# Input stage of a two-layer decoder trunk: the first pair of k-tiles in single pieces, the gain vectors on the other queue, the bias row later, the keys' scales first

## The chip, the cores and the metric

The kernel runs on one core of a Trainium2 chip. The metric is the device time of one execution in microseconds (us). Of the kernel before there are three timed runs and one profiled execution; all times below come from these.

## The reference, cut to what matters

The program is a decoder trunk on one sequence of 256 tokens with 1024 features: a DSA layer (an indexer scores the keys, the best 64 are kept, attention runs over a shared latent), an MLP, an NSA layer and a second MLP. Only its first lines bear on the change:

```
h = rmsnorm(x, g_attn[0])                 # x: 256 tokens x 1024 features
proj = h @ w_in                           # 1024 x 456
c_q, c_kv, k_idx, w_idx = split(proj, [256, 384, 448])
c_q, c_kv, k_idx = rmsnorm of each, with its own gain
rel   = relu(q_idx . k_idx)               # 8 indexer heads, queries x keys
score = sum over heads of w_idx * rel     # causal; the top 64 keys are kept
logits = q_abs . c_kv + rel_bias[bucket(distance)]   # attention, softmax
```

The norm's factor per token is applied after the product, so the kernel multiplies the raw x (times the gain of each feature) with `w_in` and scales the result later.

## The kernel before, in words

All tensors lie in SBUF in tiles of 128 partitions. The stream is held transposed (`xT`: 128 features of a k-tile on the partitions, 8 k-tiles, 256 tokens), so `w_in` is used in 8 k-tiles of 128 x 456, which arrive in four pairs (`win_raw`, 456 KB a pair; `xT`, 256 KB a pair). The result stands in two PSUM banks, `proj[0]` and `proj[1]`, one for each half of the tokens.

The first pair (j = 0) is multiplied in plain fp32: ScalarE (ACT) makes `xg` = `xT` times the gain, and TensorE (PE) runs four matmuls of 128 x 456, each of which it carries out in two passes. The pairs 1 to 3 are multiplied in split form: ACT rounds `xT` to `xgh` and `w_in` times the gain to the high half of `win`, VectorE (DVE) forms the remainders `xgl` and the low half of `win`, and PE runs three passes of 128 x 456 for each of four combinations, 12 a pair, 36 in all. The gains and some other columns lie in `vec` (26 KB).

Beside this, ACT squares `xT` into `sqs`, DVE adds the four squares, GpSimd (POOL) the last two halves (`Sx`): these are the sums for the norm of x. Behind the adds DVE copies `proj`'s first columns to `zc`, PE transposes them (`tz`), and the indexer's queries follow (`qi`). From sums of squares of `proj` (`ss`) POOL raises all scales to the power -1/2 (`scs`: column 0 for the query latent, 1 for the key latent, 2 for the indexer's keys, 3 for the norm of x). The scaled keys (`kd`, DVE) are transposed by PE (`tk`) and copied with their gain (`kiT`, DVE); PE forms the indexer's scores (`ix`), ACT cuts them at zero (`rel`), and DVE adds them up with the weights `widx` (`score`) and finds the top 64 in a long chain of MAX and MATCH_REPLACE.

The bias row is a side branch: `relb` (32 x 8) and a one-hot table `oneh` (32 x 256) are loaded on ACT's DMA queue, PE multiplies them (`ups`), DVE copies the result to `usb`, ACT's queue writes it to DRAM (`udr`), and SyncE's queue (SP) reads it back in 1 KB rows as `biasT` (1 MB), which the attention needs much later. Ahead of all products PE runs ten matmuls on a tile of ones (`warm_ps`).

The order of instructions on each engine is set by a scheduler that works on estimated times; `pin` keeps an instruction in program order among the pinned ones of its engine, `behind(a, b)` places a after b. DMA is issued by two queues, SP's and ACT's, and an issue may have to wait for a buffer: `raw` tiles come from a pool of five.

Of the kernel before, what the change touches and what calls it, by code (L numbers as in the profile page):

```python
# [22 lines left out]
F32 = mybir.dt.float32  # L23
F32R = mybir.dt.float32r
AF = mybir.ActivationFunctionType
OP = mybir.AluOpType
# [4 lines left out]
P, T, D, KT = 128, 256, 1024, 8  # L31
H, G, R, HD = 8, 2, 4, 128
# [4 lines left out]
NEG = -1e30  # L37
# [5 lines left out]
V_GA, V_GM, V_GKV, V_GF, V_GQ, V_GKVL, V_GKI = 0, 16, 32, 40, 48, 50, 51  # L43
# [7 lines left out]
def trunk(ctx: ExitStack, tc: tile.TileContext, I, out):  # L51
    nc = tc.nc
    const = ctx.enter_context(tc.tile_pool(name="const", bufs=1))
    big = ctx.enter_context(tc.tile_pool(name="big", bufs=10))
    rawp = ctx.enter_context(tc.tile_pool(name="raw", bufs=5))
# [12 lines left out]
    dram = ctx.enter_context(tc.tile_pool(name="dr", bufs=1, space=DRAM))  # L68

    def bank(name, acc=False):  # L70
        if acc:
            return psA.tile([P, 512], F32, tag="acc", name=name)
        return psB.tile([P, 512], F32, tag="ps", name=name)

    def bigt(shape, dt, name):
        return big.tile(shape, dt, tag="big", name=name)

    def wk(tag, bufs, shape, name, dt=F32):
        return work.tile(shape, dt, tag=tag, name=name, bufs=bufs)
# [4 lines left out]
    def k4(shape, name, dt=F32):  # L84
        return rawp.tile(shape, dt, tag="raw", name=name)
# [7 lines left out]
    def mm(ps, a, b, start, stop):  # L93
        return nc.tensor.matmul(ps, a, b, start=start, stop=stop, skip_group_check=True)  # L94
# [6 lines left out]
    def behind(ins, prev):  # L101

        tc.add_manual_dep(ins.ins, prev.ins.name,
                          mybir.DependencyInfo(mybir.DependencyClass.NoSync, mybir.DependencyReason.DATA),
                          reason="order")
# [98 lines left out]

    new_phase("workA")
    vec = const.tile([P, NV], F32, name="vec")
    nc.sync.dma_start(vec, I["vecs"])
    mhalf = const.tile([P, 4], F32, name="mhalf")
    nc.gpsimd.memset(mhalf, -0.5)
    ones = const.tile([P, P], F32, name="ones")  # L210
# [1 line left out]
    warm = const.tile([P, 1], F32, name="warm")  # L212
    nc.scalar.activation(warm, ones[:, 0:1], AF.Exp)
    wps = bank("warm_ps")
    for n in range(8):
        mm(wps[:, :P], ones, ones, True, True)
    relb = wk("relb", 1, [32, H], "relb")
    nc.scalar.dma_start(relb, I["rel_bias"])
    oneh = wk("pe", 4, [32, 256], "oneh")
    nc.scalar.dma_start(oneh, I["onehot"])  # L220


    ups = bank("ups")
    mm(ups[:H, :256], relb, oneh, True, True)
    for n in range(2):
        mm(wps[:, :P], ones, ones, True, True)
    usb = wk("pe", 4, [H, 384], "usb")
    nc.gpsimd.memset(usb[:, :P], NEG)
    nc.vector.tensor_copy(usb[:, P - 1:P + 255], ups[:H, :256])
    udr = dram.tile([H, 384], F32, name="udr")  # L230
    nc.scalar.dma_start(udr[:, :P + 255], usb[:, :P + 255])

    u_ap = udr[:, :]
    biasT = const.tile([P, H, T], F32, name="biasT")
# [4 lines left out]

    xT = bigt([P, KT, T], F32, "xT")
    xgh = bigt([P, KT, T], F32R, "xgh")
    xgl = bigt([P, KT, T], F32R, "xgl")
    proj = [bank(f"proj{i}", acc=True) for i in range(2)]
# [1 line left out]
    sqs = bigt([P, 4, 2, T], F32, "sqs")  # L247
    cst = const.tile([P, NC_], F32, name="cst")
    lo_last = None
    for j in range(4):  # L250
        pair = slice(2 * j, 2 * j + 2)
        nc.sync.dma_start(xT[:, pair], I["xT"][:, pair])
        raw = rawp.tile([P, 2, 456], F32, tag="raw", name=f"win{j}_raw")
        nc.sync.dma_start(raw.rearrange("p a m -> p (a m)"), I["a_w_in"][j])
        if j == 0:
            xg0 = k4([P, 2, T], "xg0")
            for k in range(2):
                nc.scalar.activation(xg0[:, k], xT[:, k], AF.Copy, scale=vec[:, V_GA + k:V_GA + k + 1])
        else:
            xh = nc.scalar.copy(xgh[:, pair], xT[:, pair])  # L260
            nc.vector.tensor_sub(xgl[:, pair], xT[:, pair], f(xgh[:, pair]))
            w = wp.tile([P, 2, 1024], F32R, tag="w", name=f"win{j}")
            wh, wl = (w[:, s, :912].rearrange("p (a m) -> p a m", a=2) for s in range(2))
            for a in range(2):
                g = vec[:, V_GA + 2 * j + a:V_GA + 2 * j + a + 1]
                hi_last = nc.scalar.activation(wh[:, a], raw[:, a], AF.Copy, scale=g)
                lo_last = nc.vector.scalar_tensor_tensor(wl[:, a], raw[:, a], g, f(wh[:, a]),
                                                         op0=OP.mult, op1=OP.subtract)
        for i in range(2):
            for a in range(2):  # L270
                k = 2 * j + a
                if j == 0:
                    mm(proj[i][:, :456], xg0[:, k, i * P:(i + 1) * P], raw[:, a], k == 0, False)
                    continue
                mm3(proj[i][:, :456], xgh[:, k, i * P:(i + 1) * P], xgl[:, k, i * P:(i + 1) * P],
                    wh[:, a], wl[:, a], False, k == KT - 1)
    for j in range(4):
        behind(nc.scalar.activation(sqs[:, j], xT[:, 2 * j:2 * j + 2], AF.Square), hi_last if j > 1 else xh)
    for j in range(1, 4):
        sq_last = nc.vector.tensor_tensor(sqs[:, 0], sqs[:, 0], sqs[:, j], op=OP.add)  # L280
        behind(sq_last, lo_last)
# [60 lines left out]
    ss = const.tile([P, 2, 4], F32, name="ss")  # L342
# [9 lines left out]
                                               accum_out=ss[:, i, j:j + 1])  # L352
        nc.vector.tensor_scalar(ss[:, i, :3], ss[:, i, :3], epv[:, i:i + 1], None, op0=OP.add)
    scs = const.tile([P, 2, 4], F32, name="scs")
    nc.gpsimd.tensor_tensor(scs[:, :, :3], ss[:, :, :3], mhalf[:, None, :3].to_broadcast([P, 2, 3]), op=OP.pow)
    pin(nc.gpsimd.tensor_tensor(scs[:, :, 3], msx, mhalf[:, :2], op=OP.pow))
    sc = [scs[:, i] for i in range(2)]
    indexer_queries(0)
# [303 lines left out]
    pe, pT, oT = {}, {}, {}  # L662
# [116 lines left out]
    for fi in range(NF):  # L779
# [21 lines left out]
        if 18 <= fi < 26:  # L801
            k = fi - 18
# [69 lines left out]
    for kv in range(2):  # L872
        ps = bank(f"kc{kv}")
        for g in range(G):
# [7 lines left out]
                                      op=OP.mult)  # L882
# [62 lines left out]
    for c in range(4):  # L945
        h, l = weights(I["kvV"][c], f"wv{c}")
        for i in range(2):
            for j in range(2):
                k = 2 * c + j
# [17 lines left out]
    raw = rawp.tile([P, 1024], F32, tag="raw", name="wg_raw")  # L967
# [244 lines left out]
    for fi in range(NF):  # L1212
# [14 lines left out]
        if 16 <= fi < 20:  # L1227
            i, c = divmod(fi - 16, 2)
# [86 lines left out]
def _pack(x, g_attn, g_mlp, w_up, w_down, rel_bias, a_w_in, a_g_q_lat, a_g_kv_lat, a_g_k_idx,  # L1315
          a_w_uq, a_w_q_idx, a_w_uk, a_w_uv, a_w_o, g_kv_shared, w_kv_shared, cmp_pos_k, cmp_pos_v,
          cmp_w1_k, cmp_w2_k, cmp_w1_v, cmp_w2_v, b_w_in, b_w_o, g_final):
    A = np.ascontiguousarray

    def col(v):  # L1320
        return v.reshape(-1, P).T

    def mtiles(w):

        K, M = w.shape
        return A(w.reshape(K // P, P, M // P, P).transpose(2, 1, 0, 3).reshape(M // P, P, K))

    def kpairs(w):

        K, M = w.shape  # L1330
        return A(w.reshape(K // 256, 2, P, M).transpose(0, 2, 1, 3).reshape(K // 256, P, 2 * M))

    c, oh, sel = _const_arrays()
    ki = a_g_k_idx[0].reshape(64, 1)
    vecs = np.concatenate([col(g_attn[0]), col(g_attn[1]), col(g_mlp[0]), col(g_mlp[1]), col(g_kv_shared),
                           col(g_final), col(a_g_q_lat[0]), col(a_g_kv_lat[0]),
                           np.concatenate([ki, ki], 0)], 1)
    wuq = a_w_uq[0].reshape(2, P, 2, 512).transpose(1, 2, 0, 3).reshape(P, 2, 1024)
    wukv = np.stack([a_w_uk[0].transpose(2, 1, 0).reshape(P, 1024), a_w_uv[0].reshape(P, 1024)], 1)
    kvw = w_kv_shared.reshape(D, 6, G, HD)  # L1340
    kT = np.concatenate([kvw[:, i, g] for i, g in ((2, 0), (4, 0), (2, 1), (4, 1), (0, 0), (0, 1), (1, 0), (1, 1))], 1)
    kV = np.concatenate([kvw[:, i, g] for i, g in ((3, 0), (3, 1), (5, 0), (5, 1))], 1)
    wq, wg = b_w_in[0][:, :H * HD], b_w_in[0][:, H * HD:]
    return {
        "xT": A(x[0].T.reshape(KT, P, T).transpose(1, 0, 2)),
        "vecs": A(vecs),
        "a_w_in": kpairs(a_w_in[0]),
        "consts": c,
        "rel_bias": A(rel_bias),
        "onehot": oh,  # L1350
        "a_w_uq": A(wuq),
        "a_w_qi": kpairs(a_w_q_idx[0].reshape(256, 512)).reshape(P, 1, 1024),
        "a_w_ukv": A(wukv),
        "a_w_o": A(a_w_o[0].reshape(H, P, D)),
        "w_up": A(np.stack([mtiles(w_up[l]) for l in range(2)])),
        "w_down": A(w_down.reshape(2, NF, P, D)),
        "kvT": mtiles(kT),
        "kvV": kpairs(kV),
        "b_w_q": mtiles(wq),
        "b_w_g": A(np.pad(wg.reshape(KT, P, 24).transpose(1, 0, 2), ((0, 0), (0, 0), (0, 8))).reshape(P, KT * 32)),  # L1360
        "pos": A(np.stack([cmp_pos_k.T, cmp_pos_v.T], 1)),
        "cmp_w1": A(np.stack([w.reshape(8, 4, P, 256).transpose(0, 2, 1, 3).reshape(8, P, 1024)
                              for w in (cmp_w1_k, cmp_w1_v)])),
        "cmp_w2": A(np.stack([w.reshape(2, P, HD).transpose(1, 0, 2) for w in (cmp_w2_k, cmp_w2_v)], 1)),
        "sel": sel,
        "b_w_o": A(b_w_o[0].reshape(H, P, D)),
        "g_final": A(np.broadcast_to(g_final, (P, D))),
    }
# [18 lines left out]
```

## Time and profile before

| | us |
|---|---|
| three timed runs, median | 593.29 (592.83 to 594.0) |
| the profiled execution's own time | 593.29 |
| its span, first to last instruction | 591.5 |
| around the span | 1.79 |
| PE busy | 577.2 (98%) |
| DVE busy | 364.2 (62%) |
| ACT busy | 320.4 (54%) |
| POOL busy | 159.1 (27%) |

The profiled execution took as long as the median run, so a sum made against it holds for the median too. The table says which engine is full on average; the change lies in the first 26 us, where that average does not decide, and the rows further down are read from there.

### The profile page before, as it was taken

To read this page: it belongs to the slowest core of one execution; us is meant where nothing else is said; L and a number is where in the kernel's file an instruction comes from. 1 tells how busy PE (TensorE), PEld (TensorE's weight loads), DVE (VectorE), ACT (ScalarE), POOL (GpSimd) and SP (SyncE) were. 2 spreads that over 40 slices of the span, in tenths; PEclk is the share of its full clock that TensorE was granted. 3 is DMA by queue.
4 is the path that set the end of the run, shared out by engine and by line. 5 is a ranking of instruction groups with operands and counts; after the bars stand their busy time and mean duration, and the time that the engine had idled before them with its cause. 6 is when DMAs were issued, how large, how long until landed. Compare 5 with 4: busy or idle time off the path is not lost.

```text
span 591.5 us, 10852 instructions
## 1 busy us (share of the span) xinstructions
PE 577.2 (98%) x4170; PEld 542.9 (92%) x4170; DVE 364.2 (62%) x612; ACT 320.4 (54%) x580; POOL 159.1 (27%) x225
## 2 busy tenths in 40 slices
PE   8899999999999999999999999999999999999995
PEld 6787899999999999999968999999899999999994
DVE  3897399544474444547897877639845444454523
ACT  6656666444444454436866878637544545454423
POOL 0155457010101011015530076808310110011012
PEclk9999999999999999999999999999999999999998
DMA  8911447765546656543499943314866665656201
GB/s 300 345 47 61 149 176 235 249 194 178 179 145 212 181 178 190 180 164 113 160 308 304 327 139 102 97 49 138 287 205 186 181 191 169 180 180 203 77 0 71
DMA packets 30475, 103.97 MB, mean 176 GB/s; under 512 B 3632, under 2 KB 5464, under 8 KB 30296
## 3 DMA queue, kind: packets, MB, share of 16 engines
q1 hardware_dynamic: 30024, 102.45, 53.7%
q10 hardware_dynamic: 400, 0.83, 0.5%
q8 instruction: 32, 0.52, 0.4%
q14 instruction: 19, 0.16, 0.1%
HBM read 102.21 MB, written 1.06 MB: 175 GB/s over the span
## 4 chain that ended last, share of the span: by engine, by line
PE 84%; DVE 9%; issue 2%; DMA 2%; ACT 1%; POOL 1%; SPq 1%; POOLq 0%; ACTq 0%; DVEq 0%
PE y L94 30%; PE u L94 28%; PE nq L94 4%; PE yb L94 3%; PE ya L94 3%; PE kk L94 2%; PE npo L94 2%; PE kc L94 1%; PE nl L94 1%; DVE c L903 1%; DMA win_raw<-in_a_w_in 1%; PE v L94 1%; PE co L94 1%; PE ix L94 1%; DMA wv_raw<-in_kvV 1%
## 5 line engine op out<-in xcount | busy, mean ns | idle before, releaser
L142 DVE TENSOR_TENSOR dn<-dn_raw,dn 128x1024 fp32r<-128x1024 f32 x64 | 80.6, 1260 | 99.2 <-ACT dn L141 99.2
L645 POOL TENSOR_TENSOR us<-ur 128x256 f32<-128x256 f32 x64 | 45.4, 711 | 282.0 <-ACT ur L642 282.0
L142 DVE TENSOR_TENSOR up<-up_raw,up 128x1024 fp32r<-128x1024 f32 x64 | 81.9, 1280 | 44.6 <-ACT up L141 44.6
L141 ACT CAST up<-up_raw 128x1024 fp32r<-128x1024 f32 x64 | 67.0, 1048 | 60.0 <-PE y L94 58.5
L94 PE MATMUL u<-h1h,up 128*128 128x256 f32 x512 | 97.0, 284 | 0.6 <-DVE up L142 0.6
L94 PE MATMUL y<-uu,dn 128*128 128x256 f32 x768 | 97.0, 283 | 0.3 <-DVE uu L647 0.3
L94 PE MATMUL u<-h0h,up 128*128 128x256 f32 x512 | 96.7, 283 | 0.0
L94 PEld LDWEIGHTS y<-uu,dn 128*128 128x128 f32 x768 | 94.2, 192 | 0.5 <-DVE uu L647 0.5
L94 PE MATMUL y<-dn,uu 128*128 128x512 f32 (+1 forms) x396 | 92.5, 384 | 0.0
L94 PEld LDWEIGHTS y<-dn,uu 128*128 128x128 f32 x396 | 71.1, 189 | 13.0
L94 PEld LDWEIGHTS u<-h1h,up 128*128 128x128 f32 x512 | 81.5, 191 | 1.6 <-DVE up L142 0.8
L642 ACT ACTIVATE ur<-u 128x256 f32<-128x256 f32 x64 | 24.6, 384 | 107.2 <-PE u L94 107.2
L94 PEld LDWEIGHTS u<-h0h,up 128*128 128x128 f32 x512 | 81.7, 192 | 0.0
L94 PE MATMUL u<-h1l,up 128*128 128x256 f32 x256 | 72.5, 283 | 0.0
L94 PE MATMUL u<-h0l,up 128*128 128x256 f32 x256 | 72.2, 283 | 0.0
L141 ACT CAST dn<-dn_raw 128x1024 fp32r<-128x1024 f32 x64 | 66.7, 1042 | 7.2 <-PE y L94 3.0
L94 PEld LDWEIGHTS u<-h1l,up 128*128 128x128 f32 x256 | 49.0, 191 | 0.9
L94 PEld LDWEIGHTS u<-h0l,up 128*128 128x128 f32 x256 | 49.1, 192 | 0.0
L647 DVE TENSOR_TENSOR uu<-us,uu 128x256 fp32r<-128x256 f32 x64 | 29.1, 455 | 8.1 <-POOL us L645 8.1
L646 ACT ACTIVATE uu<-ur 128x256 fp32r<-128x256 f32 x64 | 26.7, 417 | 0.1
L94 PE MATMUL ya<-oT,wo 128*128 128x256 f32 x192 | 25.2, 288 | 0.3 <-DVE oT L591 0.3
L94 PE MATMUL nq<-ah,wq 128*128 128x256 f32 x128 | 24.9, 286 | 0.0
(300 smaller groups left out, 966.8 us busy)
## 6 DMA issues: line engine op xcount, KB each, us to landing
up_raw<-in_w_up SPq DMA_DIRECT2D x64, 512.0 KB, 3.7
dn_raw<-in_w_down SPq DMA_DIRECT2D x64, 512.0 KB, 3.7
c1raw<-in_cmp_w SPq DMA_DIRECT2D x16, 512.0 KB, 4.9
wo_raw<-in_a_w_o SPq DMA_DIRECT2D x8, 512.0 KB, 4.1
wq_raw<-in_b_w_q SPq DMA_DIRECT2D x8, 512.0 KB, 5.9
wn_raw<-in_b_w_o SPq DMA_DIRECT2D x8, 512.0 KB, 4.9
wk_raw<-in_kvT SPq DMA_DIRECT2D x4, 512.0 KB, 3.6
wc_raw<-in_kvT SPq DMA_DIRECT2D x4, 512.0 KB, 3.6
```

Source lines behind the costliest of these rows:

```text
L94: return nc.tensor.matmul(ps, a, b, start=start, stop=stop, skip_group_check=True)
L141: ins = [hi(w[:, 0, :C], raw[:, :C]) if hi else nc.scalar.copy(w[:, 0, :C], raw[:, :C]), (lo or nc.vector).tensor_sub(w[:, 1, :C], raw[:, ...
L142: (lo or nc.vector).tensor_sub(w[:, 1, :C], raw[:, :C], f(w[:, 0, :C]))]
L642: nc.scalar.activation(r, ps[:, :T], AF.Relu)
L645: nc.gpsimd.tensor_tensor(s, r, r, op=OP.mult)
L646: nc.scalar.activation(u[:, 0], r, AF.Square)
L647: nc.vector.tensor_sub(u[:, 1], s, f(u[:, 0]))
L903: lo = nc.vector.tensor_sub(w4[:, :, 1], r4, f(w4[:, :, 0]))
```

## The change

- `vec` is loaded on ACT's queue in place of SP's, and SP starts with the first pair.
- The first pair comes in four transfers in place of two: k-tile 0 of `xT`, k-tile 0 of `w_in`, then k-tile 1 of each (128 KB and 228 KB). All input transfers are pinned in this order. The array of `xT` in DRAM is now stored pair by pair.
- The four matmuls of the first pair run k-tile by k-tile.
- The loads of `relb` and `oneh` move behind `xg`, and `ups`, `usb` and `udr` behind the products of pair 1 in the program. Ten warming matmuls stand together, and are pinned.
- The squares of pair 0 stand behind `xg`, the others behind the last high half.
- POOL's one instruction for scales 0 to 2 (128 x 6) becomes two: scale 2 first (128 x 2), then scales 0 and 1 (128 x 4).

```diff
-    nc.sync.dma_start(vec, I["vecs"])
+    pin(nc.scalar.dma_start(vec, I["vecs"]))
+    xT = bigt([P, KT, T], F32, "xT")
+    win_raw = [rawp.tile([P, 2, 456], F32, tag="raw", name=f"win{j}_raw") for j in range(4)]
+    for k in range(2):
+        pin(nc.sync.dma_start(xT[:, k], I["xT"][0, :, k * T:(k + 1) * T]))
+        pin(nc.sync.dma_start(win_raw[0][:, k], I["a_w_in"][0, :, k * 456:(k + 1) * 456]))
+    for j in range(1, 4):
+        pin(nc.sync.dma_start(xT[:, 2 * j:2 * j + 2].rearrange("p k t -> p (k t)"), I["xT"][j]))
+        pin(nc.sync.dma_start(win_raw[j].rearrange("p a m -> p (a m)"), I["a_w_in"][j]))
...
-    for n in range(8):
-        mm(wps[:, :P], ones, ones, True, True)
...
+    for n in range(10):
+        pin(mm(wps[:, :P], ones, ones, True, True))
...
+    def bias_row():
+        relb = wk("relb", 1, [32, H], "relb")
+        pin(nc.scalar.dma_start(relb, I["rel_bias"]))
+        oneh = wk("pe", 4, [32, 256], "oneh")
+        pin(nc.scalar.dma_start(oneh, I["onehot"]))
+        return relb, oneh
+    def bias_out(relb, oneh):
+        ups = bank("ups")
+        pin(mm(ups[:H, :256], relb, oneh, True, True))
+        usb = wk("pe", 4, [H, 384], "usb")
+        nc.gpsimd.memset(usb[:, :P], NEG)
+        nc.vector.tensor_copy(usb[:, P - 1:P + 255], ups[:H, :256])
+        nc.scalar.dma_start(udr[:, :P + 255], usb[:, :P + 255])
...
         if j == 0:
             xg0 = k4([P, 2, T], "xg0")
             for k in range(2):
-                nc.scalar.activation(xg0[:, k], xT[:, k], AF.Copy, scale=vec[:, V_GA + k:V_GA + k + 1])
+                xg_last = nc.scalar.activation(xg0[:, k], xT[:, k], AF.Copy, scale=vec[:, V_GA + k:V_GA + k + 1])
+            bias = bias_row()
...
-        for i in range(2):
-            for a in range(2):
+        for i, a in ((0, 0), (1, 0), (0, 1), (1, 1)) if j == 0 else ((0, 0), (0, 1), (1, 0), (1, 1)):
...
+        if j == 1:
+            bias_out(*bias)
     for j in range(4):
-        behind(nc.scalar.activation(sqs[:, j], xT[:, 2 * j:2 * j + 2], AF.Square), hi_last if j > 1 else xh)
+        behind(nc.scalar.activation(sqs[:, j], xT[:, 2 * j:2 * j + 2], AF.Square), hi_last if j else xg_last)
...
-    nc.gpsimd.tensor_tensor(scs[:, :, :3], ss[:, :, :3], mhalf[:, None, :3].to_broadcast([P, 2, 3]), op=OP.pow)
+    pin(nc.gpsimd.tensor_tensor(scs[:, :, 2], ss[:, :, 2], mhalf[:, :2], op=OP.pow))
+    pin(nc.gpsimd.tensor_tensor(scs[:, :, :2], ss[:, :, :2], mhalf[:, None, :2].to_broadcast([P, 2, 2]), op=OP.pow))
     pin(nc.gpsimd.tensor_tensor(scs[:, :, 3], msx, mhalf[:, :2], op=OP.pow))
```

The order that the scheduler makes of it differs in more than the code says. ACT at the start of the program, before (`win_134` is `win` of pair 1):

```order
L218 DMA relb<-in_rel_bias 32x8
L213 ACT_TABLE_LOAD
L213 ACTIVATE warm<-ones 128x1
L220 DMA oneh<-in_onehot 32x256
L258 ACTIVATE xg_122<-xT,vec 128x256 x2
L260 CAST xgh<-xT 128x512
L231 DMA udr<-usb 8x383
L266 ACTIVATE win_134<-win_raw,vec 128x456 x2
```

The same place of the changed kernel (`win_136` is `win` of pair 1, `xg_123` the scaled first pair):

```order
L207 DMA vec<-in_vecs 128x52
L222 ACT_TABLE_LOAD
L222 ACTIVATE warm<-ones 128x1
L270 CAST xgh<-xT 128x512
L267 ACTIVATE xg_123<-xT,vec 128x256 x2
L231 DMA relb<-in_rel_bias 32x8
L233 DMA oneh<-in_onehot 32x256
L276 ACTIVATE win_136<-win_raw,vec 128x456 x2
```

The rounding of pair 1 (`xgh`) stood behind the two instructions that scale the first pair, and now stands ahead of them; the two small loads stand between `xg` and pair 1's weights.

SP's queue at its start, before, where `vec` is first and the pairs follow in two transfers each:

```order
L207 DMA vec<-in_vecs 128x52
L252 DMA xT<-in_xT 128x512
L254 DMA win_raw<-in_a_w_in 128x912
L252 DMA xT<-in_xT 128x512
L254 DMA win_raw<-in_a_w_in 128x912
```

And in the changed kernel:

```order
L212 DMA xT<-in_xT 128x256
L213 DMA win_raw<-in_a_w_in 128x456
L212 DMA xT<-in_xT 128x256
L213 DMA win_raw<-in_a_w_in 128x456
L215 DMA xT<-in_xT 128x512
L216 DMA win_raw<-in_a_w_in 128x912
```

Pair 1 of `xT` (128x512) was the fourth transfer of the queue and is the fifth. Further down, `biasT` moves from ahead of the first `wo_raw` to behind the fourth.

DVE between the scaled keys and the first score, before:

```order
L362 TENSOR_SCALAR kd<-proj_116,scs 128x128
L370 TENSOR_SCALAR widx<-proj_115,scs 128x8
L370 TENSOR_SCALAR widx<-proj_116,scs 128x8
L372 TENSOR_SCALAR widx<-widx,scs 128x8
L367 TENSOR_SCALAR kiT<-tk,vec 64x256 x2
L372 TENSOR_SCALAR widx<-widx,scs 128x8
L379 TENSOR_TENSOR wuq_285<-wuqr_207,wuq_285 128x1024
L379 TENSOR_TENSOR wuq_288<-wuqr_208,wuq_288 128x1024
L465 SCALAR_TENSOR_TENSOR score_345<-rel_291,widx,cst 128x128
```

The same place of the changed kernel:

```order
L375 TENSOR_SCALAR kd<-proj_120,scs 128x128
L380 TENSOR_SCALAR kiT<-tk,vec 64x256 x2
L392 TENSOR_TENSOR wuq_288<-wuqr_209,wuq_288 128x1024
L392 TENSOR_TENSOR wuq_291<-wuqr_210,wuq_291 128x1024
L383 TENSOR_SCALAR widx<-proj_119,scs 128x8
L383 TENSOR_SCALAR widx<-proj_120,scs 128x8
L385 TENSOR_SCALAR widx<-widx,scs 128x8 x2
L478 SCALAR_TENSOR_TENSOR score_348<-rel_294,widx,cst 128x128
```

The small `widx` instructions stood between `kd` and `kiT` and now stand behind the two large `wuq` subtractions; nothing is left between `kd` and `kiT`. From the scores of the second half of the queries on, DVE's order is the same as before; so is PE's behind the input stage.

## Rows read from the trace of the kernel before

**Rows 1.** From the page: the chain that ended last, shares of the span by engine.
```profile
PE 84%; DVE 9%; issue 2%; DMA 2%; ACT 1%; POOL 1%; SPq 1%; POOLq 0%; ACTq 0%; DVEq 0%
```

**Rows 2.** The timeline of the first 18 us, merged: start us, length us, engine, line, operation, count, and in brackets the idle time before it and what ended it.
```profile
1.02 4.14 PE L94 MATMUL warm_ps<-ones 128*128 128x128 f32 x20 [1.02 <-POOL ones L211]
...
1.18 0.42 SPq L252 DMA_DIRECT2D xT<-in_xT  x1
...
4.95 0.91 ACT L258 ACTIVATE xg<-xT,vec 128x256 f32<-128x256 f32 x2 [2.27 <-DMA xT<-in_xT]
...
5.09 0.59 PE L94 MATMUL ups<-oneh,relb 32*8 32x256 f32 x2
...
6.34 3.30 PE L94 MATMUL proj<-win_raw,xg 128*128 128x456 f32 x8 [0.66 <-DMA win_raw<-in_a_w_in]
...
7.43 0.62 ACT L260 CAST xgh<-xT 128x512 fp32r<-128x512 f32 x1 [1.58 <-DMA xT<-in_xT]
...
9.45 1.20 PE L94 MATMUL proj<-win,xgh 128*128 128x456 f32 x3
...
10.49 0.37 PE L94 MATMUL proj<-win,xgl 128*128 128x456 f32 x1
...
17.11 0.37 PE L94 MATMUL proj<-win,xgl 128*128 128x456 f32 x1
```

**Rows 3.** The chain that ended last, in order of time, where the input stage ends: start us, length us, what.
```profile
17.49 0.67 DVE zc L314 x2
...
20.22 1.36 POOL scs L355
```

**Rows 4.** DMA in the first microseconds, from the view by stages: stretch, its length, PE busy, granted clock, mean busy share of the 16 DMA engines, GB/s.
```profile
2.00:3.00 1.00, 1.00 (x7) 1.00 0.73 161
3.00:4.00 1.00, 1.00 (x7) 1.00 0.78 162
4.00:5.00 1.00, 1.00 (x8) 1.00 0.98 371
5.00:6.00 1.00, 0.68 (x4) 1.00 0.96 279
6.00:7.00 1.00, 0.66 (x2) 1.00 0.95 307
```

**Rows 5.** DMA issues of the first 30 us: tile, queue, count, KB each, median us from issue to landing where it is known.
```profile
win_raw<-in_a_w_in SPq DMA_DIRECT2D x4, 456.0 KB, 6.4
xT<-in_xT SPq DMA_DIRECT2D x4, 256.0 KB, 5.8
...
biasT<-udr SPq DMA_DIRECT2D x1, 1024.0 KB, 10.1
...
oneh<-in_onehot ACTq DMA_DIRECT2D x1, 32.0 KB
...
vec<-in_vecs SPq DMA_DIRECT2D x1, 26.0 KB, 2.0
```

**Rows 6.** A transfer into idle DMA engines: the issue of `wo_raw` in the timeline, and the stretches behind it (length, granted clock, DMA share, GB/s). The last row is of the stretch in which the 1 KB rows of `biasT` flow (busy time of PE, PEld, DVE, ACT and POOL ahead of the granted clock).
```profile
40.24 16.46 SPq L139 DMA_DIRECT2D wo_raw<-in_a_w_o  x3
...
41.00:41.40 0.40, 1.00 0.97 143
41.40:41.80 0.40, 1.00 0.98 102
41.80:42.20 0.40, 1.00 0.47 154
42.20:42.60 0.40, 1.00 1.06 430
...
20.00:21.00 1.00, 1.00 (x6) 0.88 (x5) 0.07 (x1) 1.00 (x2) 0.78 (x1) 1.00 1.11 353
```

**Rows 7.** The timeline around the scales and the first score, and the first reader of `biasT`; columns as in rows 2.
```profile
21.54 0.70 POOL L356 TENSOR_TENSOR scs<-msx,mhalf 128x2 f32<-128x2 f32 x1
21.61 0.61 DVE L362 TENSOR_SCALAR kd<-proj,scs 128x128 f32<-128x128 f32 x2 [1.54 <-POOL scs L355]
...
22.10 0.50 PE L364 MATMUL tk<-cst,kd 128*128 128x128 f32 x2 [0.71 <-DVE kd L362]
...
22.28 0.36 DVE L370 TENSOR_SCALAR widx<-proj,scs 128x8 f32<-128x8 f32 x2
22.69 0.99 DVE L367 TENSOR_SCALAR kiT<-tk,vec 64x256 f32<-64x256 f32 x2
...
23.85 2.35 DVE L379 TENSOR_TENSOR wuq<-wuqr,wuq 128x1024 fp32r<-128x1024 f32 x2
...
26.12 0.35 DVE L465 SCALAR_TENSOR_TENSOR score<-rel,widx,cst 128x128 f32<-128x128 f32 x1
...
41.54 0.27 DVE L522 CUSTOM_DVE_ANT_0 pe<-lg,biasT 128x128 f32<-128x128 f32 x1
```

**Rows 8.** What DVE waited for between 19 and 60 us: us in total, times, longest us. The first of five rows; the other four are of waits later than 44 us.
```profile
DVE kd L362 <- POOL scs L355: 1.5, 1, 1.5
```

**Rows 9.** The end of the program by stages (busy time of PE, PEld, DVE, ACT and POOL, granted clock, DMA share, GB/s), and the weight loads of the warming matmuls (minimum, median, maximum ns).
```profile
584.00:585.00 1.00, 0.27 (x3) 0.07 (x1) 1.00 (x2) 0.30 (x2) 0.23 (x1) 1.00 0.00 0
...
588.00:589.00 1.00, 0.00 (x0) 0.00 (x0) 0.00 (x0) 0.00 (x0) 0.00 (x0) 0.58 0.89 294
...
L94 PEld LDWEIGHTS warm_ps<-ones x20: 192/333/338, 1.0 to 4.8; 128*128 128x128 f32 x20
```

More of the change, by code (lines that the diff above doesn't have):

```diff
@@ L214, in trunk @@
     wps = bank("warm_ps")
-    for n in range(8):
-        mm(wps[:, :P], ones, ones, True, True)
[L217 to L229, printed above, removed]
-    udr = dram.tile([H, 384], F32, name="udr")
-    nc.scalar.dma_start(udr[:, :P + 255], usb[:, :P + 255])
+    for n in range(10):
+        pin(mm(wps[:, :P], ones, ones, True, True))
+    udr = dram.tile([H, 384], F32, name="udr")
+    def bias_row():
[11 more added lines that the diff above has]
+        nc.scalar.dma_start(udr[:, :P + 255], usb[:, :P + 255])
     u_ap = udr[:, :]
@@ L238, in bias_keys @@
         return biasT[:, h, :ns][:, ::-1]
-    xT = bigt([P, KT, T], F32, "xT")
     xgh = bigt([P, KT, T], F32R, "xgh")
@@ L251, in trunk @@
         pair = slice(2 * j, 2 * j + 2)
-        nc.sync.dma_start(xT[:, pair], I["xT"][:, pair])
-        raw = rawp.tile([P, 2, 456], F32, tag="raw", name=f"win{j}_raw")
-        nc.sync.dma_start(raw.rearrange("p a m -> p (a m)"), I["a_w_in"][j])
+        raw = win_raw[j]
         if j == 0:
@@ L1344, in _pack @@
     return {
-        "xT": A(x[0].T.reshape(KT, P, T).transpose(1, 0, 2)),
+        "xT": kpairs(x[0].T),
         "vecs": A(vecs),
```

## The prediction, before the result was known

> **What bounds the kernel now.** I read the chain that ended last first: 84% of the span is PE [rows 1]. With PE busy in 98% of the span, what starts PE's work later starts nearly all that follows later, and the change lies ahead of all of it. So I read the first 26 us in the timeline.
>
> The first product starts at 6.34, when its pair of `w_in` has landed; `xT` came before it, and ACT had scaled both k-tiles from 4.95 to 5.86. From 6.34 PE has work up to the last product, which starts at 17.11 and is 0.37 long, so it ends at 17.48 [rows 2]. DVE's copies `zc` follow at 17.49 in the chain, 0.67 for two, then the scales of POOL, 1.36 [rows 3]. From `kd` on, DVE waits for nothing up to 44 us: the wait for the scales is its only one between 19 and 44 [rows 8]. So three things set the end: when the first product starts, how long PE needs from there to `zc`, and what DVE does behind the scales.
>
> **The change, part by part.** *ACT's order decides the first product.* In the changed order the rounding of pair 1, `xgh`, stands ahead of `xg`. ACT works in order, so `xg`, though its data come early, waits for pair 1 of `xT` and for the rounding; PE's first product waits for `xg`. Before, pair 1 of `xT` ended ACT's wait at 7.43 [rows 2], 1.09 behind the first product.
>
> When does it land now? Ahead of it and with it there were 26 + 33 + 256 + 456 + 256 = 1,027 KB, the 33 being `oneh` and the 1 KB of `relb` [rows 5]; that is 1.05 MB. Summed from 2 us on, the engines had moved 0.97 MB by 6.00 and so reached 1.05 MB at about 6.25 [rows 4]: the landing lies some 1.2 behind the bytes. Now the 33 KB go later, which takes 0.1 off, and SP's first large issue is in the place of `vec`, so it comes earlier by at most 0.45, one issue of 0.42 and the gap to the next, at 0.73 instead of 1.18 [rows 2]. The pieces of the first pair have rows of 1.0 and 1.8 KB. Value: 7.43 - 0.1 - about 0.3 = 7.05, most of the earlier start kept. The two ends: early, if the data flow as behind an idle queue. There the issue was at 40.24, first bytes at about 41.0, 0.16 MB in the next 1.2, then 430 GB/s [rows 6]; for 1.02 MB that is 0.73 + 0.76 + 1.2 + 2.0 = 4.7, and 1.2 for the landing: 5.9. Late, if nothing of the earlier start is kept and the short rows cost: 353 GB/s in the stretch of 1 KB rows [rows 6] against some 400 is 0.25 for the 0.73 MB of the first pair: 7.6.
>
> *First product.* 7.05 + 0.62 for `xgh` + 0.46 for one half of `xg` [rows 2] + a release = 8.15, in place of 6.34: 1.8 later. The pieces themselves (k-tile by k-tile, one by one) then gain nothing, since the first product waits for a transfer behind all four of them.
>
> *PE from there.* The eight passes of the first pair took 6.34 to 9.45 = 3.1. Then there are 36; three start before 10.49, so 32 steps lie between 10.49 and the last start at 17.11, 0.207 each, and 36 passes with the end of the last are 7.6 [rows 2]. The small wait that PE had in between goes, because ACT and DVE now have the weights of pair 1 ready while PE is still at the first pair: ACT reaches them at about 9.0 behind `xg`, and PE at 11.25. New in this stretch is `ups`, 0.59 for its two passes, which used to lie ahead of the first product [rows 2]; about 0.4 of it stands in the stream, its end overlapping the next pass. Sum: 8.15 + 3.1 + 7.6 + 0.4 = 19.25, against 17.48. `ups` waits for `oneh`, which is issued at about 8.5 behind a full queue, where transfers took 5.8 to 6.4 to land [rows 5]: about 14.9, and PE reaches `ups` behind 20 of the 36 passes, at 15.4. Behind it on PE wait the last 16 products, and on DVE `usb` two of the adds for `Sx`; by these numbers neither waits.
>
> *`zc`.* The second copy starts behind the last product, 19.3, and is half of 0.67 long: it ends at 19.65, against 18.16 [rows 3]. So 1.5 later, and all that hangs on it with it: the transposes, `qi`, the sums of squares and the scales.
>
> *The keys' scales.* One instruction of 128 x 6, 1.36 long [rows 3], becomes 128 x 2 first. The same operation on 128 x 2 took 0.70 [rows 7], so `kd` comes 0.65 earlier behind the sums. PE sat idle for 0.71 before `tk` [rows 7], so `tk` follows it by nearly as much. But DVE decides behind it. Before, it filled the time up to `kiT` with `widx`, 22.28 to 22.69, and then did `kiT` 0.99 and `wuq` 2.35, and the first score began at 26.12, with no wait [rows 7]. Now `kiT` follows `kd` and waits for `tk` alone, and the `widx` pieces come behind `wuq`: 20.96 for `kd` instead of 21.61, `tk` at 21.45 to 21.95, `kiT` 22.05 to 23.05, `wuq` to 25.35, `widx` about 0.65, first score about 26.0 (all on the old clock). Gain: 0.1. The ends: 0, and 0.65 if PE and not DVE decides. I take 0.1, since rows 8 show DVE without a wait from there on. The scale of the queries comes 0.35 later by the third instruction on POOL (0.70 + about 1.0 against 1.36); `zc` is scaled on ACT behind `qiT` anyway.
>
> *The rest of it.* `vec` on the other queue: it landed after 2.0 [rows 5], and `xg` now waits far longer for `xgh`, which hides it; alone it would have to come 5 later to matter. The two DMA issues between `xg` and pair 1's weights lie on ACT, about 0.4 each, within the 2.2 that ACT is ahead of PE. `biasT` is issued behind a `wo_raw` that waits for the first `wuq` subtraction, at about 26; with the 10.1 that it took before [rows 5] it lands at 36, and the first reader comes at 41.54 [rows 7] plus the shift. The squares moved on ACT lie behind the last weights, and DVE's adds end at about 18, under the products.
>
> *Sum.* +1.5 for `zc`, -0.1 for the scales: +1.4 on the profiled execution's span of 591.5 and the 1.8 around it, 593.29, which is the median as well. From there to the end nothing starts earlier by itself. I predict **594.7**. With the landing at 5.9 and 7.6 and the scales at 0.65 and 0, the ends without another mechanism are 593.0 and 595.3; the middle of these cases is 594.1 to 595.1.
>
> **The rivals.** *TensorE's clock falls in the new gap.* The warming matmuls end at 5.16, `ups` no longer follows, and PE sits idle to 8.15, 3.0 instead of 0.66 [rows 2]. At the end of the program PE stops at 584.3, the granted clock still reads 1.00 up to 588, and the stage 588 to 589 has 0.58, on the way to half, 1.2 of 2.4 GHz [rows 9]: a fall about 3.9 behind the last product. Our gap is shorter, but not by much. Price: at the start of the program the weight loads of `warm_ps` took 333 ns and at its end 192 [rows 9], over a stretch of about 3; the same slow stretch on the first pair's passes costs about half of 3.1, 1.5, and the time is 596.2; up to 597.8 if the whole first pair runs at half speed. Against it: the gap is shorter than the one after which the fall is seen.
>
> The Trainium skill, in its page "TensorE: Matmul & The Clock Gate", section "HAM oscillation — how this bites in real kernels", says that waits for transfers between groups of matmuls bring the clock down, so that each next group starts cold; by this rule the time would be this rival's 596.2. The end of this trace agrees that an idle PE loses its clock, and shows that 3.9 passed first.
>
> *The early landing hides most of it.* Pair 1 of `xT` lands near 5.9, the first product starts at 7.0, PE ends 1.15 earlier than in my sum: 593.5. For it: the front of SP's queue no longer holds the short rows of `vec`, and rows 4 show 161 GB/s in 2 to 4 us that 430 [rows 6] would beat. Against: the first 1.2 at the idle queue went at 100 to 150 GB/s too.
>
> *Faster.* The scales are worth 0.65, because PE decides behind them, and the transfers come without the slow first stretch, at 430 GB/s from 1.5 on: 1.5 + 2.4 + 1.1 (the lag of the first `xT`, by rows 2 and 4) is a landing at 5.0. The transfers decide: the point of balance is a landing at 5.65, 1.4 before my 7.05; at 5.0 it is 592.65, and with the scales' other 0.55 592.1. Against: no stretch of these rows starts at that rate.
>
> *`ups` waits.* If `oneh` lands later than 15.4, the last 16 products wait as long; one such landing 2 later than the slowest of rows 5 gives 596.2.
>
> **How the numbers follow.** A measurement of this kernel tells about 0.2%, 1.2 us, from no change, so the bounds are 592.1 and 594.5. My forecast (first product 1.2 to 2.4 later, clock kept): 0.61, of it 0.39 above 594.5 and 0.22 within. The clock falls: 0.14, slower. Early landing: 0.13, within. Faster: 0.08, of it 0.05 below 592.1 and 0.03 within. `ups` waits: 0.04, slower. Together: faster 0.05, same 0.38, slower 0.57. The range takes in the early landing and the price of one slow stretch: 593.3 to 596.3.
>
> **What would show it.** Right: ACT's `xgh` as its first instruction behind `warm`, released by `xT`; the first product at about 8.15, released by `xg`; the last at about 19.2; `zc` near 19.3; `kd` about 0.7 behind the start of the first scales; the first score near 27.5; `biasT` without a reader that waits. Wrong: a first product before 7.2; passes of the first pair longer than 0.39 (the clock); PE idle before `ups`; DVE waiting between `wuq` and the scores.

## The result, and the profile after

The changed kernel takes 597.54 us in the median of four runs (596.49 to 599.28), the kernel before 593.35 (592.83 to 594.0): a ratio of 1.0064, 95% interval 1.0048 to 1.0081. It is slower by 0.6%, by 4.2 us. I had predicted slower, but only 594.7, and the result lies above the range that ended at 596.3.

| | before | after |
|---|---|---|
| profiled execution | 593.29 | 596.49 |
| its span | 591.5 | 594.7 |
| first product starts | 6.34 | 8.17 |
| last product ends | 17.48 | 21.37 |
| first score | 26.12 | 29.61 |

The profiled execution of after is the fastest of its four. What follows explains its 3.2 us; the median has 1.05 more.

The page's busy times and its chain that ended last, the answer to [rows 1]:

```profile
PE 579.0 (97%) x4170; PEld 543.9 (91%) x4170; DVE 363.5 (61%) x612; ACT 319.7 (54%) x580; POOL 159.2 (27%) x226
PE 85%; DVE 9%; issue 2%; ACT 1%; POOL 1%; DMA 1%; SPq 0%; ACTq 0%; POOLq 0%; DVEq 0%
```

PE has the same work as before and is busy 1.8 longer (577.2 to 579.0): work that lasts longer, not only work that begins later. The timeline of after, with the columns of [rows 2], shows both:

```profile
1.02 4.61 PE L94 MATMUL warm_ps<-ones 128*128 128x128 f32 x20 [1.02 <-POOL ones L220]
...
7.09 0.62 ACT L270 CAST xgh<-xT 128x512 fp32r<-128x512 f32 x1 [4.41 <-DMA xT<-in_xT]
7.61 0.90 ACT L267 ACTIVATE xg<-xT,vec 128x256 f32<-128x256 f32 x2
8.17 5.03 PE L94 MATMUL proj<-win_raw,xg 128*128 128x456 f32 x8 [2.54 <-ACT xg L267]
...
12.68 1.15 PE L94 MATMUL proj<-win,xgh 128*128 128x456 f32 x3
...
17.27 0.59 PE L94 MATMUL ups<-oneh,relb 32*8 32x256 f32 x2
...
20.99 0.84 DVE L325 COPY zc<-proj 128x256 f32<-128x256 f32 x2 [1.22 <-PE proj L94]
21.00 0.37 PE L94 MATMUL proj<-win,xgl 128*128 128x456 f32 x1
```

The first half of the story is there as predicted. ACT waits 4.41 for pair 1 of `xT`, rounds it, and scales the first pair only then; PE stands for 2.54 behind `xg`. The second half is in the row of `proj<-win_raw,xg`: from its start to that of the next pair's passes, 12.68, it is 4.5, where before it was 3.1 [rows 2]. The view by stages says why. Columns: stretch, its length, busy time of PE, PEld, DVE, ACT and POOL, granted clock, DMA share, GB/s.

```profile
7.00:8.00 1.00, 0.00 (x0) 0.00 (x0) 0.26 (x1) 0.91 (x2) 0.00 (x0) 1.00 0.96 292
8.00:9.00 1.00, 0.83 (x2) 0.49 (x3) 0.43 (x1) 1.00 (x4) 0.00 (x0) 0.94 0.95 355
9.00:10.00 1.00, 1.00 (x3) 0.40 (x2) 0.89 (x2) 1.00 (x3) 0.00 (x0) 0.50 1.02 401
...
11.00:12.00 1.00, 1.00 (x2) 0.38 (x2) 0.73 (x3) 1.00 (x3) 0.00 (x0) 0.50 1.07 383
12.00:13.00 1.00, 1.00 (x4) 0.42 (x2) 1.00 (x2) 1.00 (x3) 0.00 (x0) 0.85 1.03 377
```

While PE idles (7 to 8) the granted clock is still 1.00, that is 2.4 GHz, and so it is when the first product starts. It falls inside the stretch 8 to 9: a mean of 0.94 means 0.12 us at half, so it falls at 8.88, 0.7 behind the start of the first product, with PE at work. It stays at 0.50, 1.2 GHz, and comes back in the stretch 12 to 13, whose 0.85 puts it at 12.30. That is 3.4 us at half speed, in which 1.7 us of work are lost. The weight loads of these products say the same (PEld in the timeline, columns as above): 0.19 us each up to 8.66, and 0.34 from 9.18 on.

```profile
8.66 0.19 PEld L94 LDWEIGHTS proj<-win_raw,xg 128*128 128x128 f32 x1 [0.19 <-issue]
9.18 0.34 PEld L94 LDWEIGHTS proj<-win_raw,xg 128*128 128x128 f32 x1 [0.34 <-issue]
```

Behind the scales DVE stands as I had put it, with two waits between the scales and the first score:

```profile
24.56 0.61 DVE L375 TENSOR_SCALAR kd<-proj,scs 128x128 f32<-128x128 f32 x2 [0.91 <-POOL scs L367]
...
25.60 1.00 DVE L380 TENSOR_SCALAR kiT<-tk,vec 64x256 f32<-64x256 f32 x2 [0.42 <-PE tk L377]
...
29.61 0.35 DVE L478 SCALAR_TENSOR_TENSOR score<-rel,widx,cst 128x128 f32<-128x128 f32 x1
```

The copy `zc` in the timeline of the kernel before, for comparison:

```profile
17.41 0.75 DVE L314 COPY zc<-proj 128x256 f32<-128x256 f32 x2
```

The wait for the scales fell from 1.54 [rows 7] to 0.91, but 0.42 of it is back as a wait for `tk`. From the start of `zc` to the first score it is 8.62, before it was 8.71 (17.41 to 26.12): 0.09 is left of the earlier scale. The first score comes 3.49 later. At 270 us, where the chain that ended last reaches the products `kk` in both kernels (before, then after: start, length), the lateness is the same, 3.48, and at the end of the span it is 3.2.

```profile
269.73 7.20 PE kk L94 x60
273.21 7.20 PE kk L94 x60
```

### The profile page after: what moved, and what is told of

It is laid out like the page before. It is cut to its first block, busy times and chain, and to the rows that moved or that the text cites. A ratio compares the mean times of both kernels' runs of the same rounds, so it can differ in the third digit from the quotient of the medians.

```text
span 594.7 us, 10859 instructions
## 1 busy us (share of the span) xinstructions
PE 579.0 (97%) x4170; PEld 543.9 (91%) x4170; DVE 363.5 (61%) x612; ACT 319.7 (54%) x580; POOL 159.2 (27%) x226
## 4 chain that ended last, share of the span: by engine, by line
PE 85%; DVE 9%; issue 2%; ACT 1%; POOL 1%; DMA 1%; SPq 0%; ACTq 0%; POOLq 0%; DVEq 0%
PE y L94 30%; PE u L94 28%; PE nq L94 4%; PE yb L94 3%; PE ya L94 3%; PE proj L94 2%; PE kk L94 2%; PE npo L94 2%; PE kc L94 1%; PE nl L94 1%; DVE c L916 1%; PE v L94 1%; PE co L94 1%; DVE h0l L160 1%; DVE score L478 1%
```

## The experiments

Each kernel was timed beside the kernel before on the same chip; there the kernel before took 593.59, 593.6 and 593.94. Ratios are to it, with 95% intervals. The expectations call the kernels e1 to e8, and so do the headings.

**The changed kernel with more warming (e2).** The order on ACT stays as changed, the first product stays late, only the gap on PE is filled.

```diff
-    for n in range(10):
+    for n in range(18):
         pin(mm(wps[:, :P], ones, ones, True, True))
```

> The changed kernel with eighteen warming matmuls in place of ten, so that PE has work up to about 7.5 us; ACT's order is left as it is. Theory A: the first product stays at about 8.2, but no stretch up to 25 us has a granted clock below 1.00, and the time is 594.7 give or take 0.4, the sum without the clock, with less spread between runs; the difference to the changed kernel, some 2.5 to 3 us, is the clock's part. Theory B': the low clock costs little and something else behind the first product is late: 596.5 or more.

Measured: 594.63 (593.98 to 595.11), ratio 1.0016 [1.0005, 1.0027]. PE in the timeline, one stage of PE alone (length, PE busy, granted clock, DMA share, GB/s), and `kk` in the chain:

```profile
1.02 7.22 PE L94 MATMUL warm_ps<-ones 128*128 128x128 f32 x36 [1.02 <-POOL ones L220]
8.08 3.32 PE L94 MATMUL proj<-win_raw,xg 128*128 128x456 f32 x8
10.88 1.14 PE L94 MATMUL proj<-win,xgh 128*128 128x456 f32 x3
...
19.19 0.37 PE L94 MATMUL proj<-win,xgl 128*128 128x456 f32 x1
```
```profile
9.00:10.00 1.00, 1.00 (x4) 1.00 1.04 404
```
```profile
271.46 7.20 PE kk L94 x60
```

The first product starts 0.09 earlier than in the changed kernel, so the lateness is the same. But PE comes to it without a gap, the clock stays at 1.00, the eight passes take 2.8 up to 10.88, 1.7 less than in the changed kernel, and the last product ends at 19.56, 1.81 earlier. The median falls by 2.9, from 597.54 to 594.63, and stands at my sum without the clock. So the idle PE, not the late product itself or the transfers beside it, brings the clock down.

How much the clock costs is shown by the traces: at `kk` this kernel is 1.73 later than the kernel before, the changed kernel 3.48, so the slow stretch is 1.75 of that, as read above, and lateness the rest. From `kk` to the end of the span the traces of all eleven runs take 320.7 to 322.0, the kernel before 321.8 and the changed kernel 321.5: that far a single time can differ for reasons that lie behind the input stage. The medians give lateness 1.0 to 1.3 of the 4.2 us and leave 2.9 to 3.2 that go with the gap. Of these the clock is shown for 1.7; the rest was in executions without a trace. One of them, 597.59, has a mean granted clock of 0.998, no lower than the kernel before (0.996 to 0.998 in 70 of 72 executions), though a stretch of 3.4 at half would take 0.003 off the mean. So the low clock, as far as that mean tells it, does not account for all of the median, and what else the gap or the lateness costs in such an execution is open.

**The changed kernel with `xg` ahead of `xgh` on ACT (e1, and e1 again as e1b).** One rule for the scheduler; with it `ups` also moved up on PE, from behind 20 of the split passes to behind 14.

```diff
             xh = nc.scalar.copy(xgh[:, pair], xT[:, pair])
+            if j == 1:
+                behind(xh, xg_last)
```

> The changed kernel with one edit: on ACT the two instructions that scale the first pair (xg) stand ahead of the rounding of pair 1 (xgh). Theory A (ACT's order makes the first product late, and the idle PE behind the warming matmuls then loses its clock): the first product starts at about 5.5 us in place of 8.17, the granted clock stays 1.00 in the first 25 us, the last product of the input stage ends near 17.3, the time is 592.6 to 593.4. Theory B (the loss comes from the rest of the change: the transfers in pieces, the bias row's product in the middle of the others, biasT later): the time stays above 595.

> The kernel of e1 again, beside the two that build on it on the same chip: 593.0, and 0.5 to 0.7 below the kernel before.

Measured: 592.98 (592.21 to 595.32), ratio 0.9988 [0.9974, 1.0002]; and on another chip 592.89, 0.9994 [0.998, 1.0009]. The timeline of the first run:

```profile
5.02 3.47 PE L94 MATMUL proj<-win_raw,xg 128*128 128x456 f32 x8
...
7.59 0.62 ACT L270 CAST xgh<-xT 128x512 fp32r<-128x512 f32 x1 [1.62 <-DMA xT<-in_xT]
...
8.40 1.24 ACT L278 ACTIVATE win<-win_raw,vec 128x456 fp32r<-128x456 f32 x2 [0.19 <-DMA win_raw<-in_a_w_in]
9.12 1.20 PE L94 MATMUL proj<-win,xgh 128*128 128x456 f32 x3 [0.63 <-ACT win L278]
...
12.52 0.59 PE L94 MATMUL ups<-oneh,relb 32*8 32x256 f32 x2
...
17.49 0.85 DVE L327 COPY zc<-proj 128x256 f32<-128x256 f32 x2 [0.58 <-PE proj L94]
```

The whole loss is undone by this one rule. With it the four pieces do bring the first product forward, by 1.32, to 5.02. But pair 1 of `xT` lands no earlier (7.59 against 7.43 [rows 2]), PE waits 0.63 for pair 1's weights, the split products start 0.33 earlier than before, and `ups` in their midst takes that back: the first score comes at 26.11, before at 26.12 [rows 7]. So without the reversal on ACT the rest of the change is worth nothing that these runs can tell.

**The kernel before with the reversal alone (e3).** `xgh` of pair 1 ahead of `xg`; the transfers and everything else in their old order (pins, not shown below, hold the transfers in it).

```diff
+    xh1 = nc.scalar.copy(xgh[:, 2:4], xT[:, 2:4])
...
-                nc.scalar.activation(xg0[:, k], xT[:, k], AF.Copy, scale=vec[:, V_GA + k:V_GA + k + 1])
+                behind(nc.scalar.activation(xg0[:, k], xT[:, k], AF.Copy, scale=vec[:, V_GA + k:V_GA + k + 1]), xh1)
```

> The kernel before with one edit: on ACT the rounding of pair 1 stands ahead of the two instructions that scale the first pair. No other instruction moves. Theory A: the first product starts at about 8.5 in place of 6.3; PE is idle from 5.7 to 8.5, somewhat less than in the changed kernel; time 595 if the clock stays and up to 597.5 if it falls. Theory B: the order on ACT is harmless, the time is 593.3.

Measured: 597.13 (596.3 to 597.89), ratio 1.0058 [1.0038, 1.0078]. PE's timeline and its stages (columns as above):

```profile
5.59 0.67 PE L94 MATMUL ups<-oneh,relb 32*8 32x256 f32 x2
8.09 5.02 PE L94 MATMUL proj<-win_raw,xg 128*128 128x456 f32 x8 [1.83 <-ACT xg L263]
```
```profile
8.00:9.00 1.00, 0.91 (x3) 1.00 1.06 417
9.00:10.00 1.00, 1.00 (x3) 0.60 1.02 383
...
11.00:12.00 1.00, 1.00 (x3) 0.50 1.05 398
12.00:13.00 1.00, 1.00 (x3) 0.70 1.04 409
```

One edit reproduces most of the loss, 3.5 of 4.2. Here `ups` still stands in the gap, PE idles for only 1.83, and the clock falls all the same: 0.60 in the stretch 9 to 10 is a fall at 9.2, 1.1 behind the start of the first product, and 0.70 in 12 to 13 a return at 12.6, again 3.4 at half speed. The first score comes at 28.88. All six executions have a mean granted clock of 0.990 to 0.995.

**The kernel before with the split scales alone (e4).**

```diff
-    nc.gpsimd.tensor_tensor(scs[:, :, :3], ss[:, :, :3], mhalf[:, None, :3].to_broadcast([P, 2, 3]), op=OP.pow)
+    pin(nc.gpsimd.tensor_tensor(scs[:, :, 2], ss[:, :, 2], mhalf[:, :2], op=OP.pow))
+    pin(nc.gpsimd.tensor_tensor(scs[:, :, :2], ss[:, :, :2], mhalf[:, None, :2].to_broadcast([P, 2, 2]), op=OP.pow))
```

> The kernel before with one edit: the keys' scales raised first (one instruction on POOL becomes two). The sum of the prediction says that DVE decides behind the scales: kd 0.65 earlier, the first score 0.1 earlier, the time 593.2. The rival says that PE decides: the time falls by the whole 0.65, to 592.7.

Measured: 593.47 (592.41 to 594.6), ratio 0.9996 [0.9983, 1.001]. DVE's timeline:

```profile
17.84 0.75 DVE L314 COPY zc<-proj 128x256 f32<-128x256 f32 x2
...
22.44 1.00 DVE L368 TENSOR_SCALAR kiT<-tk,vec 64x256 f32<-64x256 f32 x2 [0.43 <-PE tk L365]
...
26.45 0.35 DVE L466 SCALAR_TENSOR_TENSOR score<-rel,widx,cst 128x128 f32<-128x128 f32 x1
```

From `zc` to the first score it is 8.61 here and 8.71 in the kernel before: a gain of 0.1, the term of the sum. DVE stands idle for 0.43 in front of `kiT`, and nothing is left to fill that.

**The bias row early (e5).** With `xg` first as above, the loads of `relb` and `oneh` go right behind `vec` on ACT's queue, and `ups` behind the first pair's products, where PE had waited 0.63. Would PE's wait take up the 0.59 of `ups`?

```diff
+    bias = bias_row()
     xT = bigt([P, KT, T], F32, "xT")
...
-        if j == 1:
+        if j == 0:
             bias_out(*bias)
```

> The kernel of e1 with one more edit: relb and oneh are loaded at the start behind vec, and the bias row's product ups stands on PE right behind the first pair's products, where PE waits 0.6 for the weights of pair 1, in place of the middle of pair 2's. Theory (ups costs PE about 0.45 where e1 and the change have it, and nothing ahead of pair 1): zc 0.3 to 0.4 earlier than in e1, the time 592.6. Rival (the stage ends with DVE's adds or with pair 1's landing, which the two loads make later by 0.1 or more): as e1, 593.0.

Measured: 593.24 (592.25 to 595.35), ratio 0.9994 [0.9981, 1.0006]. One line of ACT:

```profile
8.98 1.24 ACT L279 ACTIVATE win<-win_raw,vec 128x456 fp32r<-128x456 f32 x2 [0.75 <-DMA win_raw<-in_a_w_in]
```

`ups` ran at 8.67, in the wait, but ACT had the weights of pair 1 only 0.6 later than with `xg` first alone (8.98 against 8.40), and the split products started at 9.70. The first score came at 26.03. The gap was used, but the later weights opened a new one.

**The first `wuq` subtraction into DVE's gap (e6).** As the one above, with one of the two large subtractions between `kd` and `kiT`.

```diff
+        sub = nc.vector.tensor_sub(w[:, 1], wuqr[j], f(w[:, 0]))
+        behind(sub, prev)
...
+    half, sub0 = wuq_half(0, kd_last)
...
         kiT_last = nc.vector.tensor_scalar(kiT[pa, a], tk[pa, :T], vec[pa, V_GKI:V_GKI + 1], None, op0=OP.mult)
+        behind(kiT_last, sub0)
```

> The kernel of e5 with one more edit: DVE does the first wuq subtraction between kd and kiT, where it waits 0.4 for PE's tk. Theory (DVE decides behind the keys' scales, and the scales' gain is lost in that wait): the first score 0.4 earlier than in e5, the time 592.2. Rival (PE decides, and kiT 0.7 later holds up ix): as e5 or up to 0.3 slower.

Measured: 592.56 (591.43 to 593.02), ratio 0.9977 [0.9968, 0.9987]. DVE in the timeline:

```profile
17.27 0.77 DVE L328 COPY zc<-proj 128x256 f32<-128x256 f32 x2
...
21.35 1.22 DVE L382 TENSOR_TENSOR wuq<-wuqr,wuq 128x1024 fp32r<-128x1024 f32 x1
...
25.35 0.35 DVE L488 SCALAR_TENSOR_TENSOR score<-rel,widx,cst 128x128 f32<-128x128 f32 x1
```

From `zc` to the first score it is 8.08, 0.53 less than with the scales alone, and the median is 0.68 below the one above, though the two intervals just overlap. The early scale is worth something when DVE has work for the time until `tk`. The same subtraction without the early scale was not tried.

**The bias row late (e7).** With `xg` first, `ups` behind the first scores of the indexer, its copy on ACT, and the read of `biasT` behind it.

```diff
-        nc.vector.tensor_copy(usb[:, P - 1:P + 255], ups[:H, :256])
+        nc.scalar.copy(usb[:, P - 1:P + 255], ups[:H, :256])
...
-        if j == 1:
-            bias_out(*bias)
...
     index_scores(0, 2)
+    bias_out(*bias)
```

> The kernel of e1 with the bias row's product ups behind the first indexer scores (ix) on PE, its copy on ACT, and biasT read later; the small loads stay behind xg. Theory (in e1 the stage ends with PE, and ups costs it 0.45 there): the last product and zc 0.45 earlier than in e1, the first score too, 592.5. Rival (DVE or the weights' landing ends the stage): as e1, 592.9; or slower, if biasT comes too late for its first reader at 41.5.

Measured: 592.46 (591.86 to 593.17), ratio 0.9975 [0.9965, 0.9986]. The timeline:

```profile
16.64 0.85 DVE L323 COPY zc<-proj 128x256 f32<-128x256 f32 x2 [0.16 <-PE proj L94]
16.65 0.37 PE L94 MATMUL proj<-win,xgl 128*128 128x456 f32 x1
...
24.70 0.59 PE L94 MATMUL ups<-oneh,relb 32*8 32x256 f32 x2
25.26 0.35 DVE L479 SCALAR_TENSOR_TENSOR score<-rel,widx,cst 128x128 f32<-128x128 f32 x1
```

With `ups` out of the stream the last product starts 0.46 earlier than before [rows 2], and the first score comes 0.86 earlier [rows 7]. `zc` starts 0.85 and 0.68 earlier than in e1 and e1b, about the 0.7 that `ups` costs in the stream (worked out further down).

**Both together (e8).** The late bias row and the subtraction in DVE's gap.

> The kernel of e7 with the first wuq subtraction between kd and kiT, as in e6. Theory: both gains add, the first score near 24.9, 592.0, and clearly below both kernels of this study. Rival: one of them is lost again behind the other engine, 592.5.

Measured: 592.49 (591.4 to 594.07), ratio 0.9969 [0.9955, 0.9983]: no faster than either alone. The profiled execution was the slowest of the six, 594.07, and shows the clock again: the weights of pair 1 came late in it (ACT scaled them at 9.02), PE waited 1.76, and the granted clock fell behind the wait (columns as in the stages of after; it reads 0.50 in the three stretches between these two).

```profile
9.74 1.21 PE L94 MATMUL proj<-win,xgh 128*128 128x456 f32 x3 [1.76 <-ACT win L278]
```
```profile
10.00:11.00 1.00, 0.95 (x4) 0.54 (x4) 1.00 (x3) 1.00 (x3) 0.00 (x0) 0.91 1.02 392
...
14.00:15.00 1.00, 1.00 (x5) 0.89 (x5) 1.00 (x3) 1.00 (x3) 0.00 (x0) 0.89 1.02 393
```

That is a fall at 10.82, 1.1 behind the resumption, and a return at 14.22: again 3.4 at half. The other five executions took 591.4 to 592.73 at a mean granted clock of 0.997 to 0.998, this one 0.993. From `zc` to the first score it is 8.11 in this trace (18.98 to 27.09) and 8.62 in e7, so in the stage both gains are there; whether they add in the time is open.

## Why the prediction was wrong

**What failed is the choice on the clock.** I listed the fall as a rival at 0.14 and left it out of the sum. The argument against it was that this gap, 3.0 by my reckoning, is shorter than the 3.9 that passed at the end of the program before the clock fell [rows 9]. (It was 2.54: the warming matmuls ended at 5.63, not at 5.16.) That row shows one gap after which the clock fell, and it does not show that a shorter one is safe. Nor is 3.9 a fixed time. Read in the same way, from the last product of the program to the fall, the eleven traces give from 1.9, in e2, to 5.3, in e1b. In e2 PE stops at 585.57 (timeline), and the mean of 0.73 in the stretch behind puts the fall at 587.46 (columns as in the stage of e2):

```profile
574.82 10.75 PE L94 MATMUL y<-dn,uu 128*128 128x512 f32 x58
```
```profile
587.00:588.00 1.00, 0.00 (x0) 0.73 1.02 410
```

What the trace of the kernel before could have told me lies elsewhere in it: PE waits 1.26 at 304 us, and the granted clock stays 1.00 (stage with all engines).

```profile
305.31 0.73 PE L94 MATMUL v<-wv,sh 128*128 128x512 f32 x2 [1.26 <-ACT wv L141]
```
```profile
304.00:305.00 1.00, 0.06 (x1) 0.00 (x0) 1.00 (x1) 0.79 (x1) 1.00 (x1) 1.00 0.97 360
```

Between 1.26 and 3.9 this kernel had no gap to decide it. Three traces now have one, of 2.54, 1.83 and 1.76, and the clock fell behind each. I had read the 3.9 as the idle time that it takes; the row tells only when the fall came. Behind these three gaps it came after PE had resumed, 0.7, 1.1 and 1.1 into the new products, and took 3.4 of running work at half speed.

The Trainium skill, "TensorE: Matmul & The Clock Gate", section "HAM oscillation — how this bites in real kernels", was right here in its direction, that a wait ahead of a group of matmuls costs the clock, for the waits of 1.76 and more. It says that the next group starts cold; in these traces it starts at full clock and turns slow under way.

**Its price was about right for the profiled execution, in part by luck.** The rival said 1.5 for one slow stretch, 596.2 in all; the stretch cost 1.7, and the execution took 596.49. But I took the half speed and its length, about 3, from the slow weight loads at the start of the program [rows 9], where the granted clock reads 1.00 [rows 4]. That a fall in the gap would last about as long, 3.4, stood in no row. In the medians the difference is 2.9, inside the 1.5 to 3.1 that I gave; the 1.2 above the 1.7 is not shown to be the clock's. The range reached to 596.3 because I took the lower price into it. What the three executions without a trace did in their further 1.0 to 2.8 us is open.

**The rest of the sum held in the main.** The landing of pair 1: 7.05 predicted, 7.09 seen. So close a hit is luck, since with the same order on SP's queue ACT had pair 1 of `xT` at 6.99 in e2 and at 7.59 in e1. First product: 8.15 and 8.17, released by `xg`. Last product without the clock: end at 19.25 predicted, 19.56 in the kernel with more warming. There the first pair's passes took 2.8 in place of my 3.1, and the other 36 with `ups` 8.7 in place of my 8.0, two misses that cancel in part. Of the 0.7 half is `ups`, which costs 0.7 in the stream and not 0.4: behind the pass at 15.16 the next two start at 15.98 and 16.30, where two steps are 0.41. The other half is the small wait that I struck out: the first three split passes take 0.97 there, as against 1.04 before. The scales: 0.1 in the sum and 0.1 in the run that tried them alone, with DVE deciding, as [rows 8] had shown. `ups` did not wait for `oneh`: no wait stands before it. Among DVE's waits up to 64 us there is none for `biasT`.

The total without the clock, 594.7, was measured as 594.63. This too is closer than the sum was: the first score of that kernel came at 27.80 in place of my 27.5, 1.7 later than before, and the time grew by only 1.0 to 1.3.

**The other rivals.** The early landing and the gain of 0.65 from the scales did not come. What I had not thought of is that the scales are worth half a microsecond (8.61 to 8.08) once other work of DVE is put in front of `kiT`.

## What to carry to other kernels

Look first at what the new order on each engine puts ahead of the instruction that starts the chain: a rounding for a later transfer, ahead of the scaling for an earlier one, made nearly the whole loss here (3.5 us when tried alone), and one rule to the scheduler gives it back. Count a new gap on TensorE as the wait plus the slow stretch that may follow it, and fill it with idle matmuls if the wait can't be removed; here eight of them gave back 2.9 of 4.2 us. When an input arrives earlier, find the next thing that is late: here pair 1's weights, then `ups` in the stream, then DVE's gap.

## What the runs showed of the hardware

The granted clock was 1.00 through each gap between products and at the resumption. It fell to 0.50 0.7, 1.1 and 1.1 us into the new work and came back 3.4 us later, alike behind gaps of 2.54, 1.83 and 1.76. Shorter gaps left it at 1.00: 0.63 in e1, 0.66 before the first product of the kernel before [rows 2], 1.26 at 304 us in the same trace, and 1.47 at the same place in e5. What decides between 1.47 and 1.76 was not tried.

At the start of the program the granted clock reads 1.00 although the weight loads of the warming matmuls take 333 ns in the median, and the shortest in the changed kernel 285, against 192 for the shortest before [rows 9]. Of the first product's loads in the changed kernel those at a granted clock of 1.00 took 0.19 us and those at 0.50 took 0.34, so in these first microseconds that column seems not to show the speed.

Pair 1's weights were scaled by ACT at 8.98 and 8.82 in the two kernels that load `relb` and `oneh` right behind `vec` on ACT's queue, and at 8.40, 8.21 and 8.26 in three runs without: 0.6 for 33 KB, of which the bytes explain 0.1 at the 400 GB/s of that stretch. Two runs without these loads, e2 and e8, had 9.09 and 9.02, though, so the landing varies by this much of itself, and no effect of the small loads is shown.
